# Conditioning rows loaded a step ahead, a later output norm and a new order of the three split products in a hybrid decoder block

## The chip, the cores and the metric

The kernel runs on one core of a Trainium2 chip. The metric is the device time of one execution in microseconds (us). The kernel before took 1613.56 us as the median of three runs, which lay between 1611.21 and 1615.91.

## What is computed

One decoder layer on 1024 tokens of width 1024, in fp32. Cut to its skeleton, the reference is:

```python
mod = silu(c) @ w_ada + b_ada                       # 6 rows of 1024
shift1, scale1, gate1, shift2, scale2, gate2 = split(mod, 6)
h = rms_norm(x, norm1_w) * (1 + scale1) + shift1
q, k, v, r, a_lr, su, sv, g_a, g_b = split(h @ w_in)
o = gla_chunked(q, k, v, log_a(a_lr))               # 4 heads, chunks of 64
o = rms_norm(o, gla_norm_w) * silu(r)               # norm over each head's 256 values
s = spatial_gating(gelu(su), gelu(sv), ...)         # layer norm, 128-token mixing
x = x + gate1 * ((sigmoid(g_a) * o + sigmoid(g_b) * s) @ w_out)
h2 = rms_norm(x, norm2_w) * (1 + scale2) + shift2
x = x + gate2 * peer(h2, w_q, keys, expert_down, expert_up)   # 8 heads x top 16 of 16384 experts
return rms_norm(x, final_norm_w)
```

`mod` is a conditioning vector: one row of 1024 numbers for each of shift, scale and gate. The change touches the way in which four of these six rows are made, the norm of `o`, and the order of the matrix products.

## The kernel before

The tokens are worked on in two halves of 512. In each half the kernel runs fourteen groups of 512 output columns of `h @ w_in` and then the `w_out` and `w_q` products. The second half runs beside the experts of the first half (the "peer stream"), which are gathered by indirect DMA.

**A weight tile.** `stream` (L1142 to L1165) goes through the eight 128-row slices k of a group's weights. For each, SyncE (SP) issues the load of `wt`, 128x512 fp32; ScalarE (ACT) rounds it to the reduced fp32 of the TensorE (`wh`, the high part, L1156); GpSimd (POOL) or VectorE (DVE) subtracts to get the low part (`wl`, L1158). In the first half DVE makes the low part of k = 0 and k = 4, in the second that of every even k; POOL makes the others. The activations are split the same way into `hTh` and `hTl`. Twelve matmuls follow: for each of four PSUM banks, the three products of `mm3` (L178 to L181): high by high (L179), then the other two (L180 and L181). Which of the two is the product with the weights' low part depends on which operand is stationary: L180 where the weights are stationary ("feat" groups, rows `mm<-wl,hTh`), L181 where the activations are.

**The side work.** After the matmuls of a weight tile, `step` advances a set of queues of Python generators by a step each. `qa` holds the conditioning rows, at a rate of 1.0 step a tile; `qm` holds the output norm and some other elementwise work; others hold the expert work. What a generator issues between two `yield`s is written into the program at that place.

**A conditioning row.** `ada_row(c, r)` (L1043 to L1057) runs four times, in the first half only. `ada_acc` (L1000 to L1010) loads eight tiles `wada` of 512 KB through SP's queue and sums them on DVE into `adacc` (L1007, then L1009), load and sum in the same step. Two empty steps later ACT's queue loads the bias (L1046), two matmuls sum over the partitions (L1050), DVE adds the bias (L1051), for the row r = 1 it also multiplies by the second norm's weights (L1055), and ACT's queue stores the row to a scratch tensor `rows_d` (L1056) at once. `rows_d` is read after the fourteen groups. All these tiles, and the four tiles `ot` of the attention output, come from one pool, `b4`, of eight buffers.

**The output norm.** After the last attention head `rso` holds the sums of squares; DVE scales them (L171) and POOL raises them to the power -1/2 (L172). `out_norm` (L1350 to L1356) then has sixteen DVE operations on 128x256 tiles `ot` (L1354), one a step. The first use of their result is the evacuation of the r groups. The groups around it run in this order: Q and K of heads 2 and 3, attention of these heads beside the groups SV0 and SV1 (columns of `sv`), then R0, R1 (columns of `r`), A0, A1, SU0, SU1, B0, B1.

**The order of the instructions.** The program is built by a framework that keeps an order of instructions per engine and decides it itself, by simulating a timeline while it builds: an instruction that is ready early in that simulation may be put ahead of others on its engine. So a change in the code's order changes the engine orders elsewhere too.

## Time and profile before

| | |
|---|---|
| median of 3 runs | 1613.56 us (1611.21 to 1615.91) |
| the profiled execution, its own time | 1611.35 us |
| its span in the profile | 1609.3 us, 20188 instructions |
| busy: TensorE (PE) | 1421.2 us (88%), 6076 matmuls |
| busy: DVE | 1093.7 us (68%) |
| busy: POOL | 833.4 us (52%) |
| busy: ACT | 772.6 us (48%) |
| HBM traffic over the span | 224 GB/s |

A share is that of the whole span; it mixes stages with different limits. The times in a timeline are counted from the span's start, and the two columns ahead of an engine's name are start and duration. A bracket at the end of a row tells how long the engine had been idle and what released it; "x4" stands for four instructions in a row whose time is summed up. The table by stretches gives busy time and number of instructions per engine, the clock that TensorE was granted (1.00 is full speed), the share of DMA time and GB/s.

### The profile page before, as it was taken

Reading aid. Unit: us, or ns where it says so; the run is one execution under the profiler, and the core shown is the slowest. Engines: PE = TensorE matmul, PEld = TensorE weight load, DVE = VectorE, ACT = ScalarE, POOL = GpSimd, SP = SyncE. Lnnn points to the kernel's source line nnn. Section 1 sums busy time; section 2 is a strip of 40 time slices with the busy share of each in tenths; the row PEclk is TensorE's granted clock in tenths of the full one; section 3 lists DMA queues with packets and bytes.
Section 4 is the critical chain, followed back from the end, with each engine's and each line's share of the span. In section 5 each row is a group of like instructions: output and inputs, shape, how many; then the busy total and the mean of one; then the engine's idle time right before and its main releaser. Section 6 shows DMA issues by size and latency. Waiting matters only on the chain.

```text
span 1609.3 us, 20188 instructions
## 1 busy us (share of the span) xinstructions
PE 1421.2 (88%) x6076; PEld 1067.0 (66%) x6076; DVE 1093.7 (68%) x2777; ACT 772.6 (48%) x1677; POOL 833.4 (52%) x682
## 2 busy tenths in 40 slices
PE   5999989999998998898988889998879997778984
PEld 3777757888777786576766667876658764345542
DVE  7664654111446698977788787878787875787782
ACT  4554333332446454745445566556555553445541
POOL 5331247643275455645666688555666563434331
PEclk7999989999999999899999999999999999989998
DMA  9643633224377556737856787956777778978972
GB/s 318 231 143 112 190 125 112 92 85 137 100 247 255 173 167 219 271 99 249 293 181 206 258 302 262 367 190 209 274 268 263 251 275 316 368 293 316 393 292 83
DMA packets 123335, 361.48 MB, mean 225 GB/s; under 512 B 16761, under 2 KB 27257, under 8 KB 107346
## 3 DMA queue, kind: packets, MB, share of 16 engines
q0 software_dynamic: 30336, 175.39, 29.4%
q1 hardware_dynamic: 70272, 132.15, 25.0%
q10 hardware_dynamic: 22610, 52.58, 9.3%
q8 instruction: 49, 0.80, 0.2%
q14 instruction: 68, 0.56, 0.1%
HBM read 335.22 MB, written 24.85 MB: 224 GB/s over the span
## 4 chain that ended last, share of the span: by engine, by line
PE 47%; DVE 21%; DMA 14%; issue 7%; ACT 6%; POOL 4%; ACTq 0%; SPq 0%; DVEq 0%; POOLq 0%
PE mm L180 10%; PE mm L181 10%; PE mm L179 10%; PE acc L564 7%; DMA wada<-in_w_ada_dram 3%; DMA uv<-in_tab_dram,ix 3%; DVE vl L573 2%; DMA uv<-in_tab_dram,dix 2%; DVE uv L542 2%; PE hps L540 2%; DVE wl L1158 1%; DMA uvd<-in_up_dram,dix 1%; PE hps L541 1%; DMA uvd<-in_down_dram,dix 1%; POOL wl L1158 1%
## 5 line engine op out<-in xcount | busy, mean ns | idle before, releaser
L1158 POOL TENSOR_TENSOR wl<-wt,wh 128x512 fp32r<-128x512 f32 x257 | 374.1, 1461 | 355.8 <-ACT wh L1156 320.3
L180 PE MATMUL mm<-wl,hTh 128*128 128x512 f32 x896 | 367.4, 410 | 10.0 <-DVE wl L1158 5.1
L179 PE MATMUL mm<-wh,hTh 128*128 128x512 f32 x896 | 342.7, 412 | 27.2 <-ACT wh L1156 7.7
L1156 ACT ACTIVATE wh<-wt 128x512 fp32r<-128x512 f32 x368 | 227.2, 626 | 281.4 <-PE mm L181 163.8
L181 PE MATMUL mm<-wh,hTl 128*128 128x512 f32 x896 | 361.2, 406 | 0.2 <-DVE hTl L1115 0.2
L179 PEld LDWEIGHTS mm<-wh,hTh 128*128 128x128 f32 x896 | 173.1, 194 | 79.0 <-ACT wh L1156 12.2
L1158 DVE TENSOR_TENSOR wl<-wt,wh 128x512 fp32r<-128x512 f32 x111 | 105.0, 946 | 159.8 <-ACT wh L1156 155.4
L180 PEld LDWEIGHTS mm<-wl,hTh 128*128 128x128 f32 x896 | 173.6, 194 | 56.8 <-POOL wl L1158 9.2
L181 PEld LDWEIGHTS mm<-wh,hTl 128*128 128x128 f32 x896 | 173.4, 194 | 41.7 <-issue 1.3
L179 PE MATMUL mm<-hTh,wh 128*128 128x512 f32 (+1 forms) x448 | 168.1, 377 | 10.5 <-ACT vt L1203 5.3
L487 POOL DMA_INDIRECT uv<-in_tab_dram,ix x92 | 98.5, 1070 | 150.5 <-PE tps L511 35.2
L180 PE MATMUL mm<-hTl,wh 128*128 128x512 f32 (+1 forms) x448 | 164.3, 368 | 0.0
L181 PE MATMUL mm<-hTh,wl 128*128 128x512 f32 (+1 forms) x448 | 159.8, 370 | 1.3 <-DVE wl L1158 0.9
L542 DVE SCALAR_TENSOR_TENSOR uv<-uv,hps 128x512 f32<-128x512 f32 x144 | 95.0, 682 | 38.3 <-PE hps L541 21.0
L573 DVE SCALAR_TENSOR_TENSOR vl<-uv,r,vh 128x512 fp32r<-128x512 f32 x92 | 89.1, 999 | 37.9 <-ACT vh L572 37.9
L179 PEld LDWEIGHTS mm<-hTh,wh 128*128 128x128 f32 x448 | 86.1, 193 | 26.9 <-ACT vt L1203 7.7
L181 PEld LDWEIGHTS mm<-hTh,wl 128*128 128x128 f32 x448 | 85.3, 192 | 16.3 <-DVE wl L1158 1.5
L180 PEld LDWEIGHTS mm<-hTl,wh 128*128 128x128 f32 x448 | 86.2, 192 | 14.0 <-issue 0.7
L564 PE MATMUL acc<-uv,W 128*128 128x512 f32 x184 | 91.0, 618 | 1.4 <-ACT W L557 1.2
L564 PE MATMUL acc<-uv,Wd 128*128 128x512 f32 x128 | 66.0, 655 | 28.1 <-ACT Wd L502 24.3
L540 PE MATMUL hps<-hh,E 128*128 128x512 f32 x144 | 72.3, 508 | 14.4 <-DVE uv L542 7.1
L564 PEld LDWEIGHTS acc<-uv,Wd 128*128 128x128 f32 x128 | 24.9, 206 | 58.4 <-ACT Wd L502 33.6
(958 smaller groups left out, 2662.3 us busy)
## 6 DMA issues: line engine op xcount, KB each, us to landing
wt<-in_w_inp_dram SPq DMA_DIRECT2D x224, 256.0 KB, 3.0
wt<-in_w_qp_dram SPq DMA_DIRECT2D x80, 256.0 KB, 3.2
wada<-in_w_ada_dram SPq DMA_DIRECT2D x32, 512.0 KB, 4.5
wt<-in_w_outp_dram SPq DMA_DIRECT2D x64, 256.0 KB, 3.1
wada<-in_w_ada_dram SPq DMA_DIRECT2D x32, 256.0 KB, 6.0
s_d<-so ACTq DMA_DIRECT2D x32, 256.0 KB, 3.2
h2l<-h_d ACTq DMA_DIRECT2D x13, 512.0 KB, 7.3
xr<-in_x_dram ACTq DMA_DIRECT2D x8, 512.0 KB, 4.1
```

The source lines that it names most:

```text
L179: nc.tensor.matmul(ps, lh, rh, start=first, stop=False)
L180: nc.tensor.matmul(ps, lh, rl, start=False, stop=False)
L181: return nc.tensor.matmul(ps, ll, rh, start=False, stop=last).ins
L487: nc.gpsimd.indirect_dma_start(out=uv[:], out_offset=None, in_=tab, in_offset=bass.IndirectOffsetOnAxis(ap=ix, axis=0))
L540: nc.tensor.matmul(hps, Ej, hh[:, sl], start=True, stop=False)
L541: nc.tensor.matmul(hps, Ej, hl[:, sl], start=False, stop=True)
L542: nc.vector.scalar_tensor_tensor(uv[:, sl], uv[:, sl], 1.0, hps, op0=OP.mult, op1=OP.mult, accum_out=r[:, 2 + n:3 + n])
L564: nc.tensor.matmul(acc[:, sl], W, v[:, sl], start=first, stop=last)
L573: nc.vector.scalar_tensor_tensor(vl, v, r[:, 5:6], vh.bitcast(F32), op0=OP.mult, op1=OP.subtract)
L1156: nc.scalar.activation(wh, wt, AF.Identity)
L1158: eng.tensor_tensor(wl, wt, wh.bitcast(F32), op=OP.subtract)
```

## The change

There are three edits. (1) `ada_acc` issues the load of the next `wada` tile ahead of the sum of the present one; the store of a finished row comes two steps after its last sum (for r = 1 the multiplication one step after the additions); the queue `qa` runs at 0.85 step a weight tile. (2) `out_norm` lets seven steps pass before it starts, and then issues two operations a step. (3) Where the eight slices k of a group are multiplied, the slices 1 to 6 go through `mm3s`: for all four banks the product high by high and the one with the weights' high part and the activations' low part, and only then, for the four banks, the product with the weights' low part. Slices 0 and 7 keep the old order. The same holds for the `w_out` products. The work itself is the same: as many loads, sums, norm operations and matmuls.

```diff
--- before.py
+++ after.py
@@ -74,6 +74,7 @@
 DIR = 4
 RR = .5
 RA = 1.0
+RAD = .85
 NEG = -3.0e38
 TINY = 1.1754944e-38
 
@@ -174,6 +175,17 @@
     def split_psum(hi, lo, ps):
         nc.scalar.activation(hi, ps, AF.Identity)
         nc.vector.tensor_tensor(lo, ps, hi.bitcast(F32), op=OP.subtract)
+
+    def mm3s(sets, k):
+        if k in (0, KD - 1):
+            for ps, lh, ll, rh, rl, feat in sets:
+                mm3(ps, lh, ll, rh, rl, k == 0, k == KD - 1)
+            return
+        for ps, lh, ll, rh, rl, feat in sets:
+            nc.tensor.matmul(ps, lh, rh, start=False, stop=False)
+            nc.tensor.matmul(ps, *((lh, rl) if feat else (ll, rh)), start=False, stop=False)
+        for ps, lh, ll, rh, rl, feat in sets:
+            nc.tensor.matmul(ps, *((ll, rh) if feat else (lh, rl)), start=False, stop=False)
 
     def mm3(ps, lh, ll, rh, rl, first, last):
         nc.tensor.matmul(ps, lh, rh, start=first, stop=False)
@@ -940,7 +952,7 @@
                 self.pump()
 
     qa, qr, qp, qdir, qm, qf = Queue(), Queue(), Queue(), Queue(), Queue(), Queue()
-    rate = {"a": 1.0, "r": RA, "d": RD, "p": RP, "m": 1.0}
+    rate = {"a": RAD, "r": RA, "d": RD, "p": RP, "m": 1.0}
 
     def step():
         qa.pump(rate["a"])
@@ -998,15 +1010,22 @@
             return aux.tile(shape, F32, name="aux", tag="aux")
 
         def ada_acc(c):
-            acc = t4("adacc")
+            acc, wts = t4("adacc"), []
+
+            def load(k):
+                wts.append(t4("wada"))
+                nc.sync.dma_start(wts[k], w_ada[k * P:(k + 1) * P, c * D:(c + 1) * D])
+
+            load(0)
+            yield acc
             for k in range(KD):
-                wt = t4("wada")
-                nc.sync.dma_start(wt, w_ada[k * P:(k + 1) * P, c * D:(c + 1) * D])
+                if k + 1 < KD:
+                    load(k + 1)
                 if k == 0:
                     with tc.issue_after(hlast[1]):
-                        nc.vector.tensor_scalar(acc, wt, sc[:, 0:1], None, op0=OP.mult)
+                        nc.vector.tensor_scalar(acc, wts[0], sc[:, 0:1], None, op0=OP.mult)
                 else:
-                    nc.vector.scalar_tensor_tensor(acc, wt, sc[:, k:k + 1], acc, op0=OP.mult, op1=OP.add)
+                    nc.vector.scalar_tensor_tensor(acc, wts[k], sc[:, k:k + 1], acc, op0=OP.mult, op1=OP.add)
                 yield acc
 
         def ada_cols(kp):
@@ -1052,7 +1071,10 @@
             if r == 1:
                 nrow = t4("nrow")
                 nc.scalar.dma_start(nrow[0:1], n2_w)
+                yield
                 nc.vector.scalar_tensor_tensor(row_[0:1], row_[0:1], 1.0, nrow[0:1], op0=OP.add, op1=OP.mult)
+            yield
+            yield
             nc.scalar.dma_start(rows_d[r:r + 1, :], row_[0:1])
             yield
 
@@ -1165,12 +1187,11 @@
             def group(src, evac, feat, pre=None):
                 def body(k, ws, pss):
                     wh, wl = ws[0]
-                    for i in range(4):
-                        cs = slice(i * P, (i + 1) * P)
-                        if feat:
-                            mm3(pss[i], wh[:, cs], wl[:, cs], hTh[:, k], hTl[:, k], k == 0, k == KD - 1)
-                        else:
-                            mm3(pss[i], hTh[:, k, cs], hTl[:, k, cs], wh, wl, k == 0, k == KD - 1)
+                    cuts = [slice(i * P, (i + 1) * P) for i in range(4)]
+                    if feat:
+                        mm3s([(pss[i], wh[:, cs], wl[:, cs], hTh[:, k], hTl[:, k], True) for i, cs in enumerate(cuts)], k)
+                    else:
+                        mm3s([(pss[i], hTh[:, k, cs], hTl[:, k, cs], wh, wl, False) for i, cs in enumerate(cuts)], k)
 
                 stream([src], body, evac, pre)
 
@@ -1348,12 +1369,15 @@
                 glw = row("glw", gla_w)
 
             def out_norm():
+                for _ in range(7):
+                    yield
                 for i in range(BH):
                     for h in range(4):
                         o = ot[i][:, h * DV:(h + 1) * DV]
                         nc.vector.scalar_tensor_tensor(o, o, rso[:, i, h:h + 1], glw[:, h * DV:(h + 1) * DV],
                                                        op0=OP.mult, op1=OP.mult)
-                        yield
+                        if h % 2:
+                            yield
 
             qm.add(out_norm())
 
@@ -1454,9 +1478,8 @@
                     nc.scalar.dma_start(xr[i], x[t0 + i * P:t0 + (i + 1) * P, :])
 
                 def body(k, ws, pss):
-                    for m in range(4):
-                        cs = slice((2 * p + m // 2) * P, (2 * p + m // 2 + 1) * P)
-                        mm3(pss[m], hTh[:, k, cs], hTl[:, k, cs], ws[m % 2][0], ws[m % 2][1], k == 0, k == KD - 1)
+                    cuts = [slice((2 * p + m // 2) * P, (2 * p + m // 2 + 1) * P) for m in range(4)]
+                    mm3s([(pss[m], hTh[:, k, cs], hTl[:, k, cs], *ws[m % 2], False) for m, cs in enumerate(cuts)], k)
 
                 def ev(m, ps):
                     i, sl = 2 * p + m // 2, slice(m % 2 * 512, (m % 2 + 1) * 512)
```

In the changed kernel the lines have moved: the wada sum is at L1026 and L1028, the bias addition L1070, the multiplication L1075, the weights' low part L1180, the output norm L1377, the expert one-hot `E` L680; the three products of `mm3s` are L185 and L186 (weights' high part) and L188 (weights' low part).

**Order on DVE, first half, around the output norm.** `wl` here is the low part of slice 4 of group SV1, and after it the next one that DVE makes; `bst` are the statistics of `sv`, `adarow` the bias additions. Before:

```order
L1009 SCALAR_TENSOR_TENSOR adacc<-wada,sc,adacc 128x1024
L1188 BN_STATS bst<-svg 128x6
L1051 TENSOR_TENSOR adarow<-adarow,aux 1x512
L171 TENSOR_SCALAR rso<-sso 128x16
L1009 SCALAR_TENSOR_TENSOR adacc<-wada,sc,adacc 128x1024
L1051 TENSOR_TENSOR adarow<-adarow,aux 1x512
L1354 SCALAR_TENSOR_TENSOR ot<-ot,rso,glw 128x256 x16
L1158 TENSOR_TENSOR wl<-wt,wh 128x512
L1009 SCALAR_TENSOR_TENSOR adacc<-wada,sc,adacc 128x1024
L1158 TENSOR_TENSOR wl<-wt,wh 128x512
```

After:

```order
L1070 TENSOR_TENSOR adarow<-adarow,aux 1x512
L172 TENSOR_SCALAR rso<-sso 128x16
L1070 TENSOR_TENSOR adarow<-adarow,aux 1x512
L1377 SCALAR_TENSOR_TENSOR ot<-ot,rso,glw 128x256 x2
L1075 SCALAR_TENSOR_TENSOR adarow<-adarow,nrow 1x1024
L1377 SCALAR_TENSOR_TENSOR ot<-ot,rso,glw 128x256 x12
L1180 TENSOR_TENSOR wl<-wt,wh 128x512
L1026 TENSOR_SCALAR adacc<-wada,sc 128x1024
L1377 SCALAR_TENSOR_TENSOR ot<-ot,rso,glw 128x256 x2
L1028 SCALAR_TENSOR_TENSOR adacc<-wada,sc,adacc 128x1024
```

The two wada sums ahead of the norm (and, further up, those between the attention states) are gone from here, fourteen of the sixteen norm operations still stand ahead of slice 4's `wl`, and the multiplication of the row r = 1 has come between them.

**Order on DVE, second half, around the output norm.** `yd` is a sum over expert rows, `E` a one-hot matrix of the expert stream; the first `wl` of the piece before is the one of slice 4 of SV1 as well. Before:

```order
L715 SCALAR_TENSOR_TENSOR yd<-uvd,rdr,yd 128x1024
L668 TENSOR_SCALAR E<-ea,hw 128x128
L1158 TENSOR_TENSOR wl<-wt,wh 128x512
L668 TENSOR_SCALAR E<-ea,hw 128x128
L1158 TENSOR_TENSOR wl<-wt,wh 128x512
L1354 SCALAR_TENSOR_TENSOR ot<-ot,rso,glw 128x256 x14
L668 TENSOR_SCALAR E<-ea,hw 128x128
L1354 SCALAR_TENSOR_TENSOR ot<-ot,rso,glw 128x256
L516 SCALAR_TENSOR_TENSOR jk,r<-ts__6715,slot_65 128x16
L1354 SCALAR_TENSOR_TENSOR ot<-ot,rso,glw 128x256
L1158 TENSOR_TENSOR wl<-wt,wh 128x512
```

After:

```order
L727 SCALAR_TENSOR_TENSOR yd<-uvd,rdr,yd 128x1024
L680 TENSOR_SCALAR E<-ea,hw 128x128
L1377 SCALAR_TENSOR_TENSOR ot<-ot,rso,glw 128x256 x10
L1180 TENSOR_TENSOR wl<-wt,wh 128x512
L1377 SCALAR_TENSOR_TENSOR ot<-ot,rso,glw 128x256 x3
L680 TENSOR_SCALAR E<-ea,hw 128x128
L1377 SCALAR_TENSOR_TENSOR ot<-ot,rso,glw 128x256 x2
L1180 TENSOR_TENSOR wl<-wt,wh 128x512
L1377 SCALAR_TENSOR_TENSOR ot<-ot,rso,glw 128x256
L528 SCALAR_TENSOR_TENSOR jk,r<-ts__6714,slot_65 128x16
```

Ten norm operations now stand ahead of the low part of slice 4, where none stood before, and thirteen ahead of the second `E`. On POOL, the raising of `rso` to its power (L172, now L173) and the issue of the gather of `h2l` have changed places: `rso` now comes first.

**Order on PE, first half, slice 4 of SV1.** The number at the end of a name tells the buffers apart: the `mm` are the four banks, 177 and 178 the high and low part of the activations. Before:

```order
L179 MATMUL mm_1708<-wh_1809,hTh_177 128x512
L179 MATMUL mm_1709<-wh_1809,hTh_177 128x512
L179 MATMUL mm_1710<-wh_1809,hTh_177 128x512
L179 MATMUL mm_1711<-wh_1809,hTh_177 128x512
L180 MATMUL mm_1708<-wl_1810,hTh_177 128x512
L181 MATMUL mm_1708<-wh_1809,hTl_178 128x512
L180 MATMUL mm_1709<-wl_1810,hTh_177 128x512
L181 MATMUL mm_1709<-wh_1809,hTl_178 128x512
L180 MATMUL mm_1710<-wl_1810,hTh_177 128x512
L181 MATMUL mm_1710<-wh_1809,hTl_178 128x512
L180 MATMUL mm_1711<-wl_1810,hTh_177 128x512
L181 MATMUL mm_1711<-wh_1809,hTl_178 128x512
```

After:

```order
L185 MATMUL mm_1676<-wh_1769,hTh_177 128x512
L186 MATMUL mm_1676<-wh_1769,hTl_178 128x512
L185 MATMUL mm_1677<-wh_1769,hTh_177 128x512
L186 MATMUL mm_1677<-wh_1769,hTl_178 128x512
L185 MATMUL mm_1678<-wh_1769,hTh_177 128x512
L186 MATMUL mm_1678<-wh_1769,hTl_178 128x512
L185 MATMUL mm_1679<-wh_1769,hTh_177 128x512
L186 MATMUL mm_1679<-wh_1769,hTl_178 128x512
L188 MATMUL mm_1676<-wl_1770,hTh_177 128x512
L188 MATMUL mm_1677<-wl_1770,hTh_177 128x512
L188 MATMUL mm_1678<-wl_1770,hTh_177 128x512
L188 MATMUL mm_1679<-wl_1770,hTh_177 128x512
```

Four matmuls stood ahead of the first that needs the low part `wl` before, eight do so after.

## The prediction

> **What bounds the kernel now.** I read the page first, then the table by stretches, the waits, and the timelines of the two places where the output norm stands. The page's head:
>
> ```profile
> span 1609.3 us, 20188 instructions
> PE 1421.2 (88%) x6076; PEld 1067.0 (66%) x6076; DVE 1093.7 (68%) x2777; ACT 772.6 (48%) x1677; POOL 833.4 (52%) x682
> ```
>
> The span is 1609.3 us; the profiled execution took 1611.35 us, so 2.05 us lie around it, and the median of 1613.56 is 2.2 above it. TensorE is busy for 88%. The change takes no matmul away, so it can win only what TensorE waits, and what it runs at half clock. By stretches:
>
> ```profile
> 40.00:160.00 120.00, 118.27 (x538) 91.35 (x536) 72.43 (x98) 59.88 (x112) 37.79 (x35) 1.00 0.48 163
> 160.00:240.00 80.00, 70.25 (x295) 53.45 (x294) 48.83 (x80) 24.87 (x54) 28.17 (x15) 0.91 0.49 155
> 240.00:420.00 180.00, 177.55 (x793) 143.29 (x792) 43.23 (x72) 60.86 (x96) 92.10 (x67) 1.00 0.34 106
> 600.00:1240.00 640.00, 566.61 (x2511) 443.07 (x2510) 519.65 (x1101) 350.88 (x765) 411.74 (x328) 0.95 0.69 243
> 197.20:200.60 3.40, 3.40 (x10) 2.64 (x9) 1.27 (x2) 2.11 (x8) 0.00 (x0) 0.50 0.50 192
> 217.70:227.90 10.20, 6.20 (x14) 4.40 (x15) 6.99 (x16) 1.36 (x3) 9.81 (x3) 0.50 0.22 75
> 825.20:828.60 3.40, 3.15 (x7) 2.04 (x8) 3.26 (x12) 3.22 (x8) 1.80 (x4) 0.50 0.99 319
> ```
>
> Columns after the length: busy time of PE, its weight load, DVE, ACT, POOL; granted clock; DMA share; GB/s. From 40 to 160 and from 240 to 420 TensorE hardly waits and has full clock. Between them, from 160 to 240, it idles 80 − 70.25 = 9.75 us and gets 0.91 of the clock. The first of the last three rows lies behind one wait there and the second around another; the third is the same thing in the second half. What TensorE waits for from 160 to 240, engine by engine:
>
> ```profile
> 195.93 0.70 PE L1321 MATMUL gaux<-vt,at 128*128 128x256 f32 x2 [3.82 <-DVE at L1313]
> 217.55 2.00 PE L179 MATMUL mm<-wh,hTh 128*128 128x512 f32 x4 [1.93 <-ACT wh L1156]
> 223.55 0.79 PE L180 MATMUL mm<-wl,hTh 128*128 128x512 f32 x1 [4.00 <-DVE wl L1158]
> 193.79 1.45 DVE L1009 SCALAR_TENSOR_TENSOR adacc<-wada,sc,adacc 128x1024 f32<-128x1024 f32 x1 [3.84 <-DMA wada<-in_w_ada_dram]
> 195.16 0.71 DVE L1313 COPY_PREDICATED at<-amask,gaux 128x512 f32<-128x512 int32 x1
> 216.87 2.19 ACT L1156 ACTIVATE wh<-wt 128x512 fp32r<-128x512 f32 x4 [10.04 <-DVE adarow L1051]
> 216.49 6.40 DVE L1354 SCALAR_TENSOR_TENSOR ot<-ot,rso,glw 128x256 f32<-128x256 f32 x16
> 222.82 0.67 DVE L1158 TENSOR_TENSOR wl<-wt,wh 128x512 fp32r<-128x512 f32 x1
> ```
>
> The three waits, 3.82 + 1.93 + 4.00 = 9.75 us, are all of the idle time of this stretch, and each goes back to a conditioning row or the norm. The mask `at` stood on DVE behind a sum that had waited 3.84 us for its wada load. ACT's queue held the store of the finished row, and the `wh` of the next tile stood 10.04 us behind it. The low part `wl` stood behind sixteen norm operations in a row.
>
> **Part 1: the conditioning rows.** How much DVE waits for these loads:
>
> ```profile
> DVE adacc L1009 <- DMA wada<-in_w_ada_dram: 31.9, 11, 6.7
> DVE adacc L1009 <- DMA wada<-in_w_ada_dram: 19.3, 8, 3.8
> wada<-in_w_ada_dram SPq DMA_DIRECT2D x32, 512.0 KB, 4.5
> ```
>
> And TensorE's pitch in a stretch at full clock, the first and the last of sixteen matmuls in a row:
>
> ```profile
> 228.18 0.39 PE L179 MATMUL mm<-wh,hTh 128*128 128x512 f32 x1
> 231.68 0.39 PE L179 MATMUL mm<-wh,hTh 128*128 128x512 f32 x1
> ```
>
> Of the first fence, the first row is the whole span, the second 155 to 240 us (total, times, longest), the third the page's issue-to-landing time, 4.5 us. The pitch is 3.50 / 15 = 0.233 us. A load issued only when the buffer's last sum is done makes each sum wait up to 3.84 us. With the load a step ahead the sum finds its data, or nearly: a step is at least 12 matmuls of 0.233, 2.8 us, which over the rate of 0.85 is 3.3, against 4.5; so a rest of about 1.2 us a sum may stay. The order shows that this rest doesn't meet the attention of heads 2 and 3: the wada sums that stood between their states have gone. So the wait of 3.82 us goes. The wait of 1.93 goes because the store now stands two steps behind the additions; what ACT waits for then is the multiplication of row 1, which stands behind two norm operations only.
>
> The sums that were moved away land elsewhere: those of row 2 beside heads 0 and 1, those of the last row in SV1 and R0, and there the order puts bias additions and sums ahead of R0's evacuation:
>
> ```profile
> 262.89 0.50 PE L179 MATMUL mm<-wh,hTh 128*128 128x512 f32 x1 [2.45 <-DVE sg L1364]
> 209.56 1.28 DVE L1009 SCALAR_TENSOR_TENSOR adacc<-wada,sc,adacc 128x1024 f32<-128x1024 f32 x1 [3.08 <-DMA wada<-in_w_ada_dram]
> 215.89 0.67 DVE L1051 TENSOR_TENSOR adarow<-adarow,aux 1x512 f32<-1x512 f32 x1
> ```
>
> TensorE already waits 2.45 us for DVE's `sg` there. One bias addition (0.67) and two sums (1.28 each at most) now stand ahead of the first two `sg`: 3.2 at most. I take +2.5 us, with 0 as the lower end (they run while the banks are still being filled) and 5 as the upper (if a sum waits for its load as well). Beside heads 0 and 1 TensorE is the slower one (118.27 of 120 busy), so the row 2 sums cost nothing there as long as DVE keeps up; if that cover goes, each costs its 1.28, and I keep ±2.
>
> **Part 2: the output norm, first half.** The norm can begin when POOL has `rso`:
>
> ```profile
> 206.65 0.19 ACT L1326 ACTIVATION_READ_ACCUMULATOR jk<-ot 128x1 f32 x1
> 212.19 2.91 POOL L172 TENSOR_TENSOR rso<-rso,mhalf 128x16 f32<-128x16 f32 x1 [18.03 <-DVE rso L171]
> 162.35 1.20 DVE L1055 SCALAR_TENSOR_TENSOR adarow<-adarow,nrow 1x1024 f32<-1x1024 f32 x1
> 218.09 10.21 POOL L1158 TENSOR_TENSOR wl<-wt,wh 128x512 fp32r<-128x512 f32 x3 [3.00 <-ACT wh L1156]
> 205.80 1.02 PE L1050 MATMUL aux<-adacc,ones 128*1 128x512 f32 x2
> ```
>
> The last sum of squares ends at 206.84, yet POOL got its input only at 212.1, since sums that waited for loads stood ahead on DVE. Without them: 207.0, plus 2.9 on POOL is 209.9. Then by the order two norm operations, the multiplication, twelve norm operations and `wl`: 14 × 0.40 (6.40 for 16) + 1.20 + 0.67 gives 217.4. TensorE at 205.80 has two pairs for the bias (about 2.5) and, to the first product with that low part, some 40 matmuls at 0.233 (9.3): 217.6. So the wait of 4.00 goes, though by a hair; eight matmuls ahead of the low part instead of four are 0.9 of it. Its cover is that hair: if POOL's low parts come between, the norm operations take longer. In the row at 218.09 three of POOL's took 10.21 beside the sixteen of DVE, which by themselves are 6.40.
>
> With the three waits go the two stretches of half clock: 3.40 us all busy, which at full clock is 1.7, and 6.20 busy, which is 3.1 less: 4.8 together. Sum for 160 to 240: −9.75 − 4.8 = −14.5.
>
> On when the clock is halved, the row decides: it was at 0.50 from 217.70, behind a wait of only 1.93 us. The Trainium skill, "TensorE: Matmul & The Clock Gate", Part 1, says that the clock drops after an idle window of about 3.4 us; by that rule the waits of 3.82 and 4.00 alone would account for it, and the sum would be the same, as all three go.
>
> **Part 2 again: second half.** There no conditioning rows run. The order puts ten norm operations ahead of the `wl` of slice 4, which stood ahead of all of them:
>
> ```profile
> 805.61 1.21 DVE L704 SCALAR_TENSOR_TENSOR uvd<-uvd,h2d 128x1024 f32<-128x1024 f32 x1
> 808.06 3.37 POOL L172 TENSOR_TENSOR rso<-rso,mhalf 128x16 f32<-128x16 f32 x1
> 808.74 0.68 DVE L1158 TENSOR_TENSOR wl<-wt,wh 128x512 fp32r<-128x512 f32 x1
> 811.46 11.12 DVE L1354 SCALAR_TENSOR_TENSOR ot<-ot,rso,glw 128x256 f32<-128x256 f32 x14 [0.26 <-POOL rso L172]
> 809.13 1.18 PE L179 MATMUL mm<-wh,hTh 128*128 128x512 f32 x4
> 825.11 0.71 PE L540 MATMUL hps<-hh,E 128*128 128x512 f32 x1 [3.87 <-ACT ts__6734 L513]
> ```
>
> `rso` was there at 811.4; its input now stands ahead of the expert product of 1.21 on DVE, so I take 810.4. Ten operations at 0.40 and 0.68 make 815.1. TensorE asks for it after eight matmuls from 809.13, at 811.0: a wait of 4.1 us is added. The price of one operation is the open size: 0.40 in the first half, but 14 in 11.12 here, 0.79, with POOL busy. At 0.79 `wl` comes at 819.0 and the wait is 8.0. A half-clock stretch would come with it, 1.7 us as at 825. Against that, the wait of 3.87 at 825.11 and its half-clock stretch (3.15 busy, 1.6 less at full clock) can go, since norm operations no longer stand in one lump ahead of the third `E`. So +4.1 + 1.7 − 3.87 = +2 (rounded; the stretch at 825 kept, as ends −1.4 with it gone and no new one, and +8.0 + 1.7 = +9.7 with nothing saved). I take +2, with the price of 0.40: in the row before, POOL began at once behind `rso`; now the issue of a gather follows it there, so that DVE's operations come first, as in the first half.
>
> **Part 3: low part last.** Each tile's first product with the low part comes 8 matmuls in instead of 1: 7 × 0.233 = 1.6 us of slack more for DVE and POOL. It can win at most what TensorE idles ahead of these products:
>
> ```profile
> L180 PE MATMUL mm<-wl,hTh 128*128 128x512 f32 x896 | 367.4, 410 | 10.0 <-DVE wl L1158 5.1
> L181 PE MATMUL mm<-hTh,wl 128*128 128x512 f32 (+1 forms) x448 | 159.8, 370 | 1.3 <-DVE wl L1158 0.9
> ```
>
> 10.0 + 1.3 − 4.0 (counted above) = 7.3. I take −5, since a good part of it is waits of about 1 us, and slices 0 and 7 keep the old order; ends 0 and −7.3.
>
> **Sum.** −14.5 + 2.5 + 2 − 5 = −15: 1611.35 − 15 = 1596.3 for the profiled execution, and 2.2 more for the median: 1598.5.
>
> **Rivals.** *The lump stays (20%).* Fourteen of sixteen norm operations still stand ahead of the same `wl` in the first half, so the change may not do there what it says. For it: the hair above, and the price of 0.79 beside POOL. If POOL's operations get ahead of DVE's at both places, 14 × 0.79 instead of 14 × 0.40 is 5.5 us, so the 4.00 stay with their 3.1 of half clock, and the second half costs its upper end, 9.7, instead of 2: −15 + 7.1 + 7.7 = −0.2, so 1613.4, no change. Against it: in the first half POOL's low parts came behind, at 218.09, and waited, not DVE. The Trainium skill, "SBUF — State Buffer", section "SBUF: two separate sides", has this as an exclusive lock: of a DVE operation with two SBUF inputs and a GpSimd operation that reads SBUF, the one that starts first holds the shared port pair for its whole length and the other blocks. The trace agrees in the first half, where POOL's three took 10.21 and DVE's sixteen, which had begun first, 0.40 each; by that rule it would be this rival wherever POOL starts first.
>
> *The expert stream is pushed out of step (14%).* In the second half TensorE waits for DVE and ACT above all at the splits of expert rows:
>
> ```profile
> PE acc L575 <- DVE vl L573: 13.5, 13, 4.1
> PE acc L574 <- ACT vh L572: 8.9, 6, 3.5
> ```
>
> That is 22.4 us from 600 to 1240, where DVE is busy 519.65 of 640. The scheduler has put both engines' order anew there. If the new order places the splits behind norm operations and low parts so that these waits double, the sum is −15 + 22.4 = +7.4: about 1621, slower. It decides from a rise of 20 on. For it: DVE is the fullest engine after TensorE there. Against it: the DVE order is the same again soon after the norm, and low parts needed later give DVE more room, not less.
>
> **How the numbers follow.** My forecast has 66%, the lump 20%, the expert stream 14%. The range takes the sum's low end, −14.5 − 2 − 1.4 − 7.3 = −25.2, as 1588.3, and a microsecond for the spread of the runs, 1587.5; up it takes in the lump with the spread, 1615. About 0.3% (4.8 us) is what a measurement of this kernel can tell from no change. Of the forecast's 66, 64 are faster by more than that, 2 within; of the lump's 20, 4 are faster (only one of the two places), 13 within, 3 slower; of the expert stream's 14, 2, 3 and 9. That is 0.70, 0.18 and 0.12.
>
> **What would show it.** Right: from 160 to 240 us TensorE busy over 76 of 80 with a clock of 1.00, DVE's waits for wada under a third of 31.9, the `wh` behind the store gone, idle ahead of the low-part products under 3 us, and a wait of 2 to 5 us for slice 4's `wl` at about 811 of the second half. Wrong: half clock still granted in that stretch, wada waits as long as before, a wait of 8 or more at 811, or waits for `vl` and `vh` above 35 us.

## The result and the profile after

The changed kernel takes 1639.03 us (median of 5 runs, 1635.22 to 1641.71) against 1613.0 (1611.21 to 1615.91) before: ratio 1.0148, interval [1.0127, 1.0169]. It is about 24 us slower by the ratio, 26 by the medians, where 15 us faster were forecast. One execution of 2766.61 us, of the kernel called "changed, rate 1.3, lists by SP" below, is left out of its ratio; the nine others lie between 1615.78 and 1632.85. The page's head:

```profile
span 1637.3 us, 20230 instructions
PE 1441.0 (88%) x6076; PEld 1077.2 (66%) x6076; DVE 1095.2 (67%) x2777; ACT 771.1 (47%) x1676; POOL 837.7 (51%) x682
```

As many matmuls, but TensorE is busy for 20 us more: more of them ran at half clock (the clock granted over the span was 0.932, before 0.949). To see where the time went, the two kernels are laid side by side at equal work: the start of the n-th high part `wh` (there are 368), after minus before.

| weight tile n | 32 | 40 | 48 | 64 | 112 | 256 | 367 (the last) | end of the span |
|---|---|---|---|---|---|---|---|---|
| before, us | 137.9 | 178.9 | 229.0 | 277.2 | 419.0 | 924.9 | 1325.2 | 1609.3 |
| after − before, us | +2.7 | +7.8 | −0.7 | +7.9 | +8.5 | +2.3 | +10.2 | +28.0 |

So there is a gain where it was forecast (8.5 us between tiles 40 and 48), but 5 are lost just ahead of it and 8.6 just behind it; 7.9 are lost between tiles 256 and 367; and behind the last weight tile, in the stage that I call the tail, 17.8 us are lost. The forecast speaks of neither of the last two. TensorE's five largest waits from 40 to 420 us (total, times, longest), after:

```profile
PE mm L191 <- DVE q L1300: 5.9, 1, 5.9
PE mm L191 <- DVE sg L1388: 5.1, 1, 5.1
PE mm L191 <- ACT svg L1208: 3.8, 2, 3.2
PE mm L191 <- ACT vt L1224: 2.7, 2, 1.9
PE mm L188 <- DVE wl L1180: 1.1, 1, 1.1
```

The waits for `at`, for `wh` behind the store, and 2.9 of the 4.0 us for `wl` have gone, as forecast. In their place stand waits at the group boundaries: for `q` (DVE empties the banks of the Q and K group of heads 2 and 3), `svg` (SV1), `sg` (R0). The same windows of the clock and stages as before (160 to 240, then two stretches of half clock and the second half's streams):

```profile
160.00:240.00 80.00, 69.26 (x299) 54.33 (x298) 35.92 (x63) 27.09 (x60) 25.40 (x13) 0.94 0.32 104
163.50:170.30 6.80, 4.10 (x10) 3.23 (x11) 6.49 (x15) 2.15 (x4) 0.00 (x0) 0.50 0.25 78
265.90:272.70 6.80, 3.88 (x9) 3.11 (x10) 5.32 (x7) 4.09 (x7) 6.80 (x5) 0.50 0.91 327
600.00:1240.00 640.00, 571.81 (x2500) 446.76 (x2500) 522.93 (x1123) 348.49 (x757) 412.03 (x327) 0.93 0.68 241
```

Tiles 256 to 367 and the tail, first before, then after:

```profile
924.90:1325.20 400.30, 362.49 (x1677) 283.73 (x1675) 321.00 (x739) 227.55 (x498) 258.29 (x209) 0.97 0.75 266
1325.20:1609.30 284.10, 220.06 (x671) 120.61 (x669) 196.34 (x779) 124.07 (x375) 101.94 (x93) 0.91 0.76 294
927.20:1335.40 408.20, 375.10 (x1704) 294.34 (x1703) 316.94 (x763) 226.00 (x496) 260.40 (x214) 0.94 0.73 262
1335.40:1637.30 301.90, 229.13 (x659) 123.30 (x657) 196.28 (x759) 123.79 (x377) 100.77 (x90) 0.86 0.72 278
```

Stretches at half clock lie around the new waits for `q` and `sg`. From tile 256 to 367 TensorE idles less than before (33.1 us against 37.8), but is busy for 12.6 us more, at a clock of 0.94 instead of 0.97: this loss is one of clock, and where it comes from wasn't traced. In the tail its idle time grows from 64.0 to 72.8 us and its busy time by 9.1, at 0.86 instead of 0.91. What stands ahead of `q` and ahead of SV1's statistics on DVE:

```profile
161.79 1.28 DVE L1028 SCALAR_TENSOR_TENSOR adacc<-wada,sc,adacc 128x1024 f32<-128x1024 f32 x1 [0.22 <-DMA wada<-in_w_ada_dram]
163.00 1.29 DVE L1309 TENSOR_TENSOR dt<-G 128x512 f32<-128x512 f32 x2
164.20 1.28 DVE L1028 SCALAR_TENSOR_TENSOR adacc<-wada,sc,adacc 128x1024 f32<-128x1024 f32 x1
165.73 0.41 DVE L1300 SCALAR_TENSOR_TENSOR q<-mm,eG 128x256 f32<-128x256 f32 x1
...
238.18 3.03 DVE L1028 SCALAR_TENSOR_TENSOR adacc<-wada,sc,adacc 128x1024 f32<-128x1024 f32 x2 [7.30 <-DMA wada<-in_w_ada_dram]
241.12 1.28 DVE L1209 BATCH_NORM_STATS2 bst<-svg 128x6 f32<-128x512 f32 x2
```

The second row's sums run into `q`. The third row's stand ahead of the statistics `bst`: DVE waits 7.30 us for a load there and adds 3.03, so the statistics start at 241.1 instead of 234.6, and with them the layer norm of `sv`, on which ACT, with the sigmoid for R0 queued behind it, depends. In the tail, ACT and TensorE:

```profile
1397.80 0.52 ACTq L327 DMA_DIRECT2D tsh_d<-tl  x1
...
1409.50 0.40 ACT L514 ACTIVATE Wd<-ident,rd 128x128 f32<-128x128 f32 x1 [5.08 <-DMA tsh_d<-th]
...
1420.04 0.40 ACT L514 ACTIVATE Wd<-ident,rd 128x128 f32<-128x128 f32 x1 [9.72 <-DMA tsh_d<-tl]
```

```profile
1420.49 8.35 PE L576 MATMUL acc<-uv,Wd 128*128 128x512 f32 x12 [7.17 <-ACT Wd L514]
```

`tsh_d` is the scratch tensor through which ACT's queue stores the expert lists `th` and `tl` of the second half and loads them again (`thl`, `tll`). The scheduler has put these loads twelve instructions of ACT behind the later store, with eight of the 32 `Wd` still to come. The DMA is full of gathers there (396 GB/s from 1395.2 to 1419.6 us), the stores land late, and ACT holds the scaled one-hots `Wd`, for which TensorE's direct expert sums wait, for 5.08 + 9.72 us. Before the change it was seventeen instructions, the loads stood behind all but two of the `Wd`, and ACT waited 2.06 us:

```profile
1408.91 1.06 ACT L476 ACTIVATE hh<-h2l 128x1024 fp32r<-128x1024 f32 x1 [2.06 <-DMA thl<-tsh_d]
```

### The profile page after: what moved, and what is told of

Same layout as the page of the kernel before. It is cut to its first block, busy times and chain, and to the rows that moved or that the text cites. A ratio compares the mean times of both kernels' runs of the same rounds, so it can differ in the third digit from the quotient of the medians.

```text
span 1637.3 us, 20230 instructions
## 1 busy us (share of the span) xinstructions
PE 1441.0 (88%) x6076; PEld 1077.2 (66%) x6076; DVE 1095.2 (67%) x2777; ACT 771.1 (47%) x1676; POOL 837.7 (51%) x682
## 5 line engine op out<-in xcount | busy, mean ns | idle before, releaser
L1180 POOL TENSOR_TENSOR wl<-wt,wh 128x512 fp32r<-128x512 f32 x257 | 372.8, 1458 | 375.9 <-ACT wh L1178 252.9
L185 PE MATMUL mm<-wh,hTh 128*128 128x512 f32 x672 | 274.3, 411 | 2.8 <-ACT wh L1178 2.5
L186 PE MATMUL mm<-wh,hTl 128*128 128x512 f32 x672 | 272.0, 407 | 0.0
L188 PE MATMUL mm<-wl,hTh 128*128 128x512 f32 x672 | 213.5, 406 | 9.6 <-DVE wl L1180 7.7
L1180 DVE TENSOR_TENSOR wl<-wt,wh 128x512 fp32r<-128x512 f32 x111 | 97.3, 877 | 148.4 <-ACT wh L1178 95.6
L188 PEld LDWEIGHTS mm<-wl,hTh 128*128 128x128 f32 x672 | 127.8, 192 | 45.9 <-DVE wl L1180 10.5
L185 PEld LDWEIGHTS mm<-wh,hTh 128*128 128x128 f32 x672 | 131.2, 195 | 38.8 <-ACT wh L1178 6.8
L186 PEld LDWEIGHTS mm<-wh,hTl 128*128 128x128 f32 x672 | 130.4, 194 | 30.3 <-issue 0.2
L585 DVE SCALAR_TENSOR_TENSOR vl<-uv,r,vh 128x512 fp32r<-128x512 f32 x92 | 95.2, 1066 | 39.6 <-ACT vh L584 36.4
L191 PE MATMUL mm<-wh,hTh 128*128 128x512 f32 x224 | 93.2, 428 | 32.1 <-DVE q L1300 9.8
L576 PE MATMUL acc<-uv,Wd 128*128 128x512 f32 x128 | 74.2, 727 | 32.7 <-ACT Wd L514 28.3
L186 PE MATMUL mm<-hTl,wh 128*128 128x512 f32 x240 | 98.1, 409 | 0.0
L192 PE MATMUL mm<-wl,hTh 128*128 128x512 f32 x224 | 93.6, 418 | 4.2 <-POOL wl L1180 4.2
L185 PE MATMUL mm<-hTh,wh 128*128 128x512 f32 x240 | 97.0, 404 | 0.0
L191 PE MATMUL mm<-hTh,wh 128*128 128x256 f32 (+1 forms) x208 | 71.5, 346 | 9.2 <-ACT vt L1224 5.8
```

Of the source, the lines that this page charges most:

```text
L185: nc.tensor.matmul(ps, lh, rh, start=False, stop=False)
L186: nc.tensor.matmul(ps, *((lh, rl) if feat else (ll, rh)), start=False, stop=False)
L188: nc.tensor.matmul(ps, *((ll, rh) if feat else (lh, rl)), start=False, stop=False)
L191: nc.tensor.matmul(ps, lh, rh, start=first, stop=False)
L192: nc.tensor.matmul(ps, lh, rl, start=False, stop=False)
L576: nc.tensor.matmul(acc[:, sl], W, v[:, sl], start=first, stop=last)
```

## The experiments

Theory S: of edit 1 the load ahead is a gain, and the rate and the later store make the loss of the first half, as they move the sums to where DVE empties banks. It became theory R: the rows are late, whichever of their steps then stands in the way. Theory Q: the loss of the tail is that of an order in which an in-order queue waits for DMA, not of work. Against them stood that the new order of the products (P), the loads in flight (L) or the gathers themselves (G) are the cost, and that the tail only follows from the first half (F). Edit 2 by itself leaves the order of every engine word for word as it was, so it wasn't run alone. The ratios are to the kernel before, run beside each (its median was 1615.39 us beside the first four, 1614.42 beside the next four and 1617.43 beside the last four). "Lag 112" is the start of weight tile 112, against before (as in the table above), "tail" the time from the start of the last `wh` to the end of the span.

| kernel | median, us | ratio, interval | lag 112 | tail |
|---|---|---|---|---|
| before | 1613.0 | 1 | 0 | 284.1 |
| changed | 1639.03 | 1.0148 [1.0127, 1.0169] | +8.5 | 301.9 |
| edit 1 alone | 1624.46 | 1.0056 [1.0041, 1.0071] | +13.9 | 286.9 |
| edit 3 alone | 1604.25 | 0.9942 [0.9921, 0.9964] | −3.7 | 282.9 |
| changed, lists by SP | 1628.12 | 1.0083 [1.0051, 1.0115] | +9.2 | 289.5 |
| before, lists by SP | 1615.88 | 0.9998 [0.9981, 1.0015] | +2.9 | 285.4 |
| edit 3 and loads ahead | 1605.26 | 0.9949 [0.9923, 0.9975] | −5.1 | 281.9 |
| edit 3 and rate 0.85 | 1620.89 | 1.0040 [1.0014, 1.0065] | +8.0 | 284.7 |
| edit 3 and later store | 1611.99 | 0.9976 [0.9951, 1.0002] | −0.1 | 283.1 |
| changed, fewer late sums | 1615.69 (one run) | | +7.3 | 288.1 |
| changed, rate 1.2 | 1612.29 | 0.9977 [0.9949, 1.0005] | −4.9 | 284.8 |
| changed, rate 1.3 | 1624.29 | 1.0056 [1.0035, 1.0078] | −4.2 | 294.6 |
| changed, rate 1.3, lists by SP | 1625.79 | 1.0053 [1.0023, 1.0083] | −3.5 | 297.6 |
| edits 2 and 3, without 1 | 1600.81 | 0.9901 [0.9871, 0.9931] | −4.2 | 284.7 |

**Edit 1 alone, edit 3 alone.** Each is the kernel before with the hunks of that edit and nothing else:

```diff
 # edit 1, cut: the rate, ada_acc, ada_row
+RAD = .85
...
+                if k + 1 < KD:
+                    load(k + 1)
...
+            yield
+            yield
             nc.scalar.dma_start(rows_d[r:r + 1, :], row_[0:1])
```

```diff
 # edit 3, cut: mm3s in place of mm3
+                        mm3s([(pss[i], wh[:, cs], wl[:, cs], hTh[:, k], hTl[:, k], True) for i, cs in enumerate(cuts)], k)
```

> The kernel before with edit 1 alone (loads a step ahead, later store, rate 0.85). Theory Q (the loss comes from what the new engine orders do to in-order queues): from 160 to 240 us the three waits go as in the changed kernel (about -8 us there with their half clock), beside heads 0 and 1 the row's sums stand ahead of q and a wait of about 5 us for q appears as in the changed kernel, R0 adds some 2.5; in the tail nine scaled one-hots Wd stand behind the list loads on ACT (4 before the change, 12 after it), which gives +3 to +8. Sum: -3 to +8 us against before. Rival P (the order of the three products itself costs the time): without it only the gain is left, -5 to -9 us.

> The kernel before with edit 3 alone (low-part products last). Theory Q: the first half as before the change, its three waits from 160 to 240 us still there but the one for the low part shorter by about 0.9, so 0 to -3 us; in the tail seven Wd stand behind the list loads on ACT, +2 to +6. Sum: -2 to +5 us. Rival P: most of the loss of the changed kernel, +15 to +25 us.

Edit 3 is a gain of 9 us (ratio 0.9942): theory P has fallen. Edit 1 alone is a loss of 9, all of it in the first half (lag 13.9, and 7.9 at the last tile). It has the wait for `q` (5.55) and a wait of 10.21 for R0's `sg`, ahead of which DVE does three sums in 7.77 us, 2.6 each beside POOL instead of 1.28:

```profile
264.28 7.77 DVE L1017 SCALAR_TENSOR_TENSOR adacc<-wada,sc,adacc 128x1024 f32<-128x1024 f32 x3
271.97 2.47 DVE L1375 TENSOR_TENSOR sg<-mm,sg 128x512 f32<-128x512 f32 x4
```

The two effects don't add: 0.56% − 0.58% is nothing, and the changed kernel is 1.48% slower.

**The list loads by another queue**, in the changed kernel and in the one before:

```diff
-        nc.scalar.dma_start(th.bitcast(F32), ts_d[b][:, :3 * n + 2])
-        nc.scalar.dma_start(tl.bitcast(F32), ts_d[b][:, 3 * n + 2:])
+        q = nc.sync if pl["own"] else nc.scalar
+        q.dma_start(th.bitcast(F32), ts_d[b][:, :3 * n + 2])
+        q.dma_start(tl.bitcast(F32), ts_d[b][:, 3 * n + 2:])
```

> The changed kernel, with the loads of the expert lists (thl, tll) of the second half issued by SP's queue instead of ACT's. Theory Q: ACT no longer waits 5.1 and 9.7 us for the lists' stores ahead of its Wd from 1404 to 1420 us; the direct lists go on, 10 to 14 us less than the changed kernel: 1625 to 1629. Rival G (the tail is bounded by the gathers, whose DMA is full around 1400 us, and ACT's wait is hidden behind them): no change, within 3 us of 1639. Rival P also expects no change.

> The kernel before, with the same move of the list loads to SP's queue. Theory Q: there four Wd only stand behind these loads and ACT's wait for them is 2.1 us, so -3 to +1 us. Rival G: no change, within 2 us. If the move were a gain of 10 us here too, ACT's queue would be a cost of the tail that both kernels share, and no reason for the loss.

The changed kernel wins 0.65% (1.0148 to 1.0083), 10 us, most of it in the tail (301.9 to 289.5; the profiled execution is the fastest of four); the kernel before wins nothing. So which queue these loads go through costs the changed kernel time, and not the other, and rival G, which expected no change, has fallen here. That it costs by ACT's wait, for which TensorE then waits, the traces don't show. The tail with the lists by SP:

```profile
1331.60:1621.10 289.50, 217.10 (x657) 118.75 (x655) 197.03 (x759) 122.97 (x377) 99.72 (x90) 0.89 0.75 290
```

ACT's wait is gone, but TensorE idles there for 72.4 us, as in the changed kernel (72.8), and its waits for `Wd` are 27.5 us (28.3 in the changed kernel, 21.5 before). What fell is its busy time, by 12.0 us, at a clock of 0.89 instead of 0.86. 5.4 us of the tail's loss stay. DVE waits there for a row of tokens, as it does in the changed kernel (8.1) and does not before:

```profile
DVE uv L510 <- DMA h2l<-h_d: 7.6, 1, 7.6
```

**Edit 1 in pieces, on top of edit 3.** Their diffs to edit 3 alone are the hunk of `ada_acc`; the rate; the three `yield`s ahead of the store:

```diff
+    rate = {"a": .85, "r": RA, "d": RD, "p": RP, "m": 1.0}
```

```diff
+            yield
+            yield
             nc.scalar.dma_start(rows_d[r:r + 1, :], row_[0:1])
```

> Edit 3 and, of edit 1, only the load a step ahead (store at once, rate 1.0 as before). Its orders differ from those of edit 3 alone in the first half only. Theory S (of edit 1 the load ahead is a gain, and the rate and the later store make the loss by moving the sums to where DVE evacuates banks): no sum stands ahead of R0's evacuation, the three waits from 160 to 240 us go, so 2 to 6 us less than edit 3 alone (1604): 1598 to 1602. Rival L (two loads of 512 KB in flight delay the weight tiles in SP's queue, and that is the cost of edit 1): 1608 to 1616, with waits of ACT for weight tiles as in the changed kernel (8.3 and 3.5 us about 228 to 234 us).

> Edit 3 and, of edit 1, only the rate of 0.85 (loads and store as before). Theory S: the last two rows slip to SV1, R0 and R1, their sums stand ahead of and among R0's evacuations on DVE, and TensorE waits 5 to 10 us there: 1608 to 1615. Rival L: no second load in flight, so about 1604 like edit 3 alone, 1601 to 1607.

> Edit 3 and, of edit 1, only the later store. Theory S: the wh behind the store no longer waits, but little else changes, as edit 3 alone shows no such wait above 1 us on TensorE: 1601 to 1606. If the later store were the cost of edit 1, it would be 1608 or more.

The loads ahead change nothing (0.9949 against 0.9942), so neither the gain of theory S nor the cost of rival L is there. The rate costs 1% (0.9942 to 1.0040, some 16 us), more than expected, with a wait of 10.4 us for R0's `sg`:

```profile
PE mm L190 <- DVE sg L1374: 10.4, 1, 10.4
PE mm L190 <- ACT svg L1197: 5.5, 3, 3.1
```

The later store costs 0.3%, with intervals that touch (0.9921 to 0.9964, and 0.9951 to 1.0002); I had expected nothing. What the expensive pieces share is time: a row took 11 steps and 11 weight tiles, at 0.85 step a tile it takes 13, the later store makes 13 or 14 steps of it, with the loads ahead 14 or 15, and at 0.85 these are 17 tiles. The number of tiles alone doesn't give the price: 13 of them cost 16 us by the rate and some 5 by the store. Rival L was run at the old rate only.

**Fewer late sums.**

```diff
-                else:
+                elif c not in (3, 5):
                     nc.vector.scalar_tensor_tensor(acc, wts[k], sc[:, k:k + 1], acc, op0=OP.mult, op1=OP.add)
```

> The changed kernel, in which the last two conditioning rows sum only the first of their eight tiles; all loads stay. Read the first half in the profile. Theory S: the wait for R0's evacuation (5.1 us at 269 us) falls below 2.5, and the fourteen weight tiles around it win 5 to 8 us; the wait for q (5.9 us at 166) stays, since the second row's sums are still there. Rival L: both the waits for weight tiles at 228 and 234 us and the R0 stage stay as in the changed kernel. The tail of this kernel has more Wd behind the list loads on ACT than the changed one, so theory Q expects the tail no shorter, and the total between 1626 and 1640.

This kernel leaves out fourteen sums, and so computes other rows. Here my account of R0 fell in its first form. The sums are gone, but the wait for `sg` is 6.6, not below 2.5. Another step of the same row has taken the sums' place ahead of the statistics, with as long a wait for a load:

```profile
238.34 0.68 DVE L1070 TENSOR_TENSOR adarow<-adarow,aux 1x512 f32<-1x512 f32 x1 [7.38 <-DMA adarow<-in_b_ada_dram]
238.94 0.67 DVE L1209 BATCH_NORM_STATS2 bst<-svg 128x6 f32<-128x512 f32 x1
```

So it isn't the sums' 1.28 us each, but that a late row's step stands there and waits. The tail was a miss of theory Q as well: the list loads have more `Wd` behind them than in the changed kernel, and yet the tail is short (288.1). The lists are stored and loaded some 20 us earlier there (1377 to 1384 us, at 187 GB/s of DMA traffic), and ACT waits for them for no time that shows. So the number of `Wd` behind the loads doesn't set the price; that it is where the stores meet the gathers fits, but no run varies that alone.

**Rows in time.**

```diff
-RAD = .85
+RAD = 1.2
```

The second is the same with 1.3, the third the same with 1.3 and the list loads by SP, the fourth the changed kernel without any hunk of edit 1.

> The changed kernel with the conditioning rows at 1.2 steps a weight tile instead of 0.85. A row takes 14 or 15 steps since the change, 11 before it: 17 tiles at 0.85, 12 at 1.2, 11 before. Theory R (the loss in the first half is the rows' lateness): no row step stands among R0's evacuations or ahead of q, so the first half ends 4 to 8 us earlier than before the change instead of 8.5 later. Theory Q for the tail: ACT's order there has four Wd behind the list loads as before the change, so the tail costs nothing: 1600 to 1609. If the loads ahead or the later store were the cost, it would stay above 1625.

> The changed kernel at 1.3 steps a tile. Theory R: the first half as at 1.2. Theory Q: here ACT's order in the tail is that of the changed kernel (the list loads three or four instructions behind their stores, eight and more Wd behind them), so the tail loses 10 to 18 us again: 1614 to 1626. Rival F (the tail only follows from the first half): within 4 us of the kernel at 1.2.

> The changed kernel at 1.3 with the list loads on SP's queue. Theory Q: 8 to 12 us less than the same without that move. Rival F: no change, within 3 us.

> Edits 2 and 3 without edit 1. Theory R: the first half as with edit 3 alone, 3 to 8 us better than before the change. In the tail the list loads are issued early (a dozen Wd behind them, as in the kernel with fewer sums, where ACT's wait was small as the stores came ahead of the densest gathers): 0 to +6 us. The norm of the second half: -3 to +5. Sum: 1600 to 1615. If edit 2 were the loss: 1625 or more.

At 1.2 the loss is gone: 0.9977, 1.7% (27 us) below the changed kernel by one number of the code, 13 of it in the first half (lag +8.5 to −4.9) and, by the profiled executions, 17 in the tail. TensorE's waits there, to be held against those of the changed kernel:

```profile
PE mm L191 <- DVE sg L1388: 4.1, 1, 4.1
PE mm L188 <- DVE wl L1180: 3.5, 1, 3.5
PE mm L191 <- DVE q L1300: 1.2, 1, 1.2
```

At 1.3 the first half is the same (−4.2), yet the total is 0.8% worse, and the tail 9.8 us longer: rival F, that the tail only follows from the first half, has fallen. In this tail TensorE idles for 71.9 us (62.7 at 1.2), and ACT waits for the lists' stores again, 17 us in sum:

```profile
1396.95 0.20 ACT L511 ACTIVATE rd<-rd 128x1 f32<-128x1 f32 x1 [8.05 <-DMA tsh_d<-th]
1407.32 0.20 ACT L511 ACTIVATE rd<-rd 128x1 f32<-128x1 f32 x1 [9.00 <-DMA tsh_d<-tl]
```

But moving the loads to SP, which had won 10 us, wins nothing here, against theory Q and as G would have it. ACT's wait is gone, and TensorE itself waits for the same lists, with the direct sums queued behind, and DVE for 7.4 us for a row of tokens:

```profile
1401.49 0.46 PE L523 MATMUL tps<-thl,E 128*128 128x170 f32 x2 [4.04 <-DMA thl<-tsh_d]
1409.06 3.54 PE L577 MATMUL acc<-uv,Wd 128*128 128x512 f32 x4 [3.81 <-ACT Wd L515]
```

The move takes a wait off one in-order engine, others wait in its place, and TensorE's idle time in the tail stays (70.4 us). Without edit 1 the kernel is the fastest that was measured: 0.9901, interval [0.9871, 0.9931], which overlaps that of edit 3 alone, 16 us faster than before, with a tail of 284.7, in which ACT waits 0.6 us for the lists; they are stored at 1366 us, ahead of the densest gathers (199 GB/s until their loads go out, 392 in the 22 us behind). Edit 1 at 0.85 costs 2.5% on top of it.

## Why the prediction was wrong, point by point

- **What bounds the kernel, and what a wait costs**: right. The three waits from 160 to 240 us went as read, and the stretches of half clock belong to them. That edits 1 and 2 took them away is shown only in part: with edit 3 alone, which was not to touch the one for `wh`, it is gone as well, and the 4.00 for `wl` are 0.93 and 0.85. That TensorE would be busy for over 76 of the 80 us was wrong (69.26, at a clock of 0.94 instead of 1.00), since the waits for `q` and for SV1's `svg` fell into the same window.
- **"Beside heads 0 and 1 TensorE is the slower one (118.27 of 120 busy), so the row 2 sums cost nothing there as long as DVE keeps up"**: this step failed. A share of busy time over 120 us says nothing of the one moment when the banks are to be emptied. The wait for `q` rose from 1.2 to 5.9, with 6.8 us of half clock; at a rate of 1.2 it is 1.2 again.
- **R0, +2.5 us, ends 0 and 5**: this step failed too, and that the wait rose by 2.6 (2.45 to 5.07) is luck. Edit 3 alone has 4.0 there, without a late row; and DVE doesn't stand at the sums that I had priced, it waits for ACT's sigmoid:

```profile
268.07 0.69 DVE L1388 TENSOR_TENSOR sg<-mm,sg 128x512 f32<-128x512 f32 x1 [1.40 <-ACT sg L1387]
234.36 0.63 ACT L1178 ACTIVATE wh<-wt 128x512 fp32r<-128x512 f32 x1 [3.50 <-DMA wt<-in_w_inp_dram]
```

  What has no term in my sum is the third row's sum that waits 7.3 us ahead of the layer norm's statistics, at the end of the group before, SV1's wait of 3.25, and two stretches of half clock; between tiles 48 and 64 the lag grew by 8.6. SV1's wait has a cause of its own: ACT's `svg` stood behind a `wh` that waited 3.50 us for its weight tile (second row). Why that tile came late wasn't traced.
- **The rate** has no term in my sum at all, only a step's length of 3.3 us by which I argued that a load arrives in time. With the steps that edit 1 adds, it makes a row last 17 tiles instead of 11. It is the largest single cost: 1% on top of edit 3, and 1.7% between 0.85 and 1.2 in the changed kernel, of which 13 us are the first half; the rest lies in the tail, which is long again at 1.3.
- **The loads ahead, where I had seen the gain of edit 1**: no change (0.9949 against 0.9942). In the changed kernel DVE does wait less for them (21.1 us instead of 31.9, where under a third was forecast), but at worse places:

```profile
DVE adacc L1028 <- DMA wada<-in_w_ada_dram: 18.3, 7, 7.3
DVE adacc L1026 <- DMA wada<-in_w_ada_dram: 2.8, 1, 2.8
```

- **The output norm**: first half right, by a hair as said (a rest of 1.1 us for that `wl`). In the second half a wait of 4.1 was worked out, and 4.34 came, by luck: the norm's price was 0.62 an operation, between my two rows (0.40 and 0.79), 2.2 us more for the ten, and TensorE asked for the low part 2.5 us behind the norm's start instead of 0.6:

```profile
816.92 6.19 DVE L1377 SCALAR_TENSOR_TENSOR ot<-ot,rso,glw 128x256 f32<-128x256 f32 x10
823.77 2.08 PE L188 MATMUL mm<-wl,hTh 128*128 128x512 f32 x4 [4.34 <-DVE wl L1180]
```

- **The products, −5 us, ends 0 and −7.3**: the sign is right (edit 3 alone wins 9), the mechanism is not. What was to go was TensorE's idle time ahead of the products with the low part. It was 11.3 us before, is 7.8 + 3.1 + 2.5 = 13.4 with edit 3 alone, and 17.5 in the changed kernel, where under 3 were forecast. Edit 3 alone:

```profile
L187 PE MATMUL mm<-wl,hTh 128*128 128x512 f32 x672 | 213.5, 405 | 7.8 <-DVE wl L1169 7.0 <-POOL wl L1169 0.8
```

  That each tile's first such product comes eight matmuls in isn't so either: in the changed kernel's trace, of the 912 low-part products of `mm3s` (L188) only 512 stand four in a row as written; the framework has put the others between the products of the other banks. Edit 3 alone wins 6.7 us between tiles 40 and 56, where the waits of 1.93 and 4.00 shrink; the rest was not traced.
- **The rival of the lump** did not come; **the rival of the expert stream** had the right sign, but neither the place nor the wait. From 600 to 1240 the waits for `vl` and `vh` fell, 22.4 to 13.0:

```profile
PE acc L587 <- DVE vl L585: 9.1, 8, 2.7
PE acc L586 <- ACT vh L584: 3.9, 5, 1.2
```

The tail, with 17.8 us the largest loss, has no term in my sum. That it hangs on the order of the instructions is shown (9.8 us between 1.2 and 1.3 at the same first half, 9.2 of them idle time of TensorE); the one instruction that makes it is not. Another queue for the list loads wins 10 us of it in the changed kernel and nothing at 1.3, and in neither does TensorE idle less, so that ACT's wait for the lists is the cause isn't shown. Why the build's simulated timeline picks the one order or the other isn't settled; the first half's timing, the products and the rate all change it.

## What to carry to other kernels

Work that is spread over the steps of a pipeline has a length in steps: when a yield is added or a rate lowered, work out where its last step lands, and what stands behind it on that engine. Look for the in-order engine that waits for a DMA with a bank's evacuation, or the statistics for it, queued behind; the busy share of a stretch hides it. When such a wait is taken away, read the idle time of the engine that bounds the stage as well, since here it stayed. Where a scheduler fixes the order by a simulation, compare the orders to the very end, above all where a load follows a store of the same tensor, and time the edits one by one: here two of three together are 1% faster, and all three 1.5% slower.

## What the runs showed of the hardware

In the changed kernel a wait of TensorE of 1.85 us, ended at 70.3, was enough for a stretch of half clock of 3.4 us behind it, from 71.3, as 1.93 had been before the change. A store of 224 KB on ACT's queue at 1397.8 us landed only at 1419.6, 21.8 us later (by the load that waited for it), while gathers held the DMA busy (8.66 of the 9.66 MB that it moved from 1395.2 to 1419.6); the same store took less than 6 us in the kernel without edit 1 (issued at 1367.4, and its load went out at 1372.9). And with edit 1 alone a sum of 128x1024 on DVE, whose median is 1.29 us there, took 2.6 in a row of three, while POOL was busy for 6.67 of 7.70 us.
